# A Strassen stage's shared operands: four combinations moved to VectorE, four stores moved to SyncE, the plain half split first

## The chip, the cores and the metric

One core of one Trainium2 chip. The kernel computes a one-layer encoder trunk in fp32 accuracy. The metric is the device time of one execution in microseconds (us); the kernel before takes 1294.77 us in the median of three runs (1293.78 to 1295.44).

## The reference, cut to what matters

Tokens: 1024, plus 16 meta tokens; width 1024; FFN width 22 x 128 = 2816. The first half of the layer (RMSNorm, three token mixers, output projection, residual) is not touched by the change. The second half is

```python
a = rmsnorm(h, norm2)
h = h + (silu(a @ w_gate) * (a @ w_up)) @ w_down
out = rmsnorm(h, final_norm)
```

and the change lies in the operand `a` of the products with `w_gate` and `w_up`.

## The kernel before, in words

Every fp32 product is made of three fp32r products: each operand is split into a rounded part ("hi", a cast on ScalarE) and the rest ("lo", a subtraction of hi from the operand, on VectorE), and TensorE adds hi*hi, hi*lo and lo*hi. `product` (L890) does this for four blocks of 128 of the width, so one `product` is 12 matmuls of 128x512.

The activations of the FFN, transposed and scaled by `norm2`, lie in four fp32 tiles of 128 x 4 x 512: `bf[g, j]`, where g is the half of the width and j the half of the tokens. `turn_block(b)` (L740 on) makes the 128 tokens of block b: eight TensorE transposes (L744) of the normalised rows `hss[b]`, then two VectorE multiplications into `bf[0, j]` and `bf[1, j]` (L745). Blocks 4 to 7 (j = 1) come first, then blocks 0 to 3 (j = 0). `split_block(b)` makes hi (ScalarE, L751) and lo (VectorE, L752) of one block for both g; the parts are the tiles `bs[g, j]`.

Of the 22 chunks of 128 FFN columns, chunks 0 and 1 (`PAIR0`) are computed directly, `direct(c, j)`: gate and up, each `product` with `bs[0, j]` and then `bs[1, j]` into one PSUM bank of tag "s" (four banks), silu on ScalarE (L934), the multiplication with up on VectorE (L936), and a store of the result to DRAM (L924). It runs for j = 1 first, while blocks 0 to 3 are still being made, and for j = 0 afterwards. Chunks 2 to 21 go in pairs through `strassen`, seven products in place of eight on halves of the width and of the tokens. It needs, beside the plain parts `bs[0, 0]`, `bs[1, 0]`, `bs[1, 1]`, the parts t1, t2, t3, t4 of four combinations of the tiles `bf`:

- t3 = parts of bf[1,1] - bf[0,1]
- t1 = parts of bf[0,1] - bf[0,0], written in place over bf[0,1]
- t2 = parts of bf[1,1] - (the new bf[0,1]), in place over bf[1,1]
- t4 = parts of bf[1,0] - (the new bf[1,1]), in place over bf[1,0]

The four subtractions of 128 x 2048 run on GpSimd (L941, L949, L951, L953). `parts` makes hi with one cast of 128 x 2048 on ScalarE (L919) and lo with one subtraction of that size on VectorE (L920).

Where tiles lie sets what waits for what. `bs[g, 0]`, the tile of the t3 combination and the parts of t1, t2 and t3 are buffers of one tag "t" in the pool `rt`, which takes the memory of the closed pools `hp`, `x0` and `wo` (rows of the residual, normalised rows and weights of the stage before). The pool opens after block 3 has been transposed. The pool `po` of the Strassen part takes over the memory of the tiles `bf`; in it lie the raw weights of the second chunk of each pair, loaded by SyncE (L883). GpSimd adds and subtracts quarters of these raw weights (L989, L972), and ScalarE and VectorE split them (L876, L878).

The order on each engine is not written by hand. A planner goes through the program with its own estimate of each instruction's time and gives each engine the ready instruction that stands first in the program; the chip then runs each engine's list strictly in that order, and an instruction whose input is late holds up all that is behind it on its engine. A DMA is issued by the queue of the engine that the program names and waits there for its data in the same way. The buffers of one tag are handed out as the planner reaches their first writers.

Of the kernel before, what the change touches and what calls it, by code (L numbers as in the profile page):

```python
# [8 lines left out]
F32 = mybir.dt.float32  # L9
# [3 lines left out]
ALU = mybir.AluOpType  # L13
# [17 lines left out]
def hymba_trunk(  # L31
# [19 lines left out]
    nc = tc.nc  # L51
    V, S, G, PE = nc.vector, nc.scalar, nc.gpsimd, nc.tensor

    def pool(name, side=None, space=None, bufs=1):
        kw = {}
        if side is not None:
            kw["side"] = side
        if space is not None:
            kw["space"] = space
        return tc.tile_pool(name=name, bufs=bufs, reuse_waits="tile", **kw)  # L60
# [3 lines left out]
    def T(p, shape, dt, tag, bufs=1):  # L64
        uid[0] += 1
        return p.tile(list(shape), dt, tag=tag, bufs=bufs, name=f"{tag}_{uid[0]}")
# [689 lines left out]
    wts, bf, bs, hss, last_y = {}, {}, {}, {}, {}  # L756
# [3 lines left out]
    gsd = [dpool.tile([128, SEQ], F32, name=f"gsd{c}") for c in range(2)]  # L760
# [94 lines left out]
    g = len(OGROUPS) - 1  # L855
# [16 lines left out]
    HB = [128, 4, 512]  # L872
# [42 lines left out]
    rt = rt_stack.enter_context(pool("rt", side="right"))  # L915

    def parts(p, tag, bufs, a):
        hi, lo = [T(p, HB, F32R, tag, bufs) for _ in range(2)]
        S.copy(hi, a)  # L919
        V.tensor_tensor(lo, a, hi, ALU.subtract)  # L920
        return hi, lo

    def store(c, j, g):
        nc.scalar.dma_start(gsd[c][:, 512 * j:512 * j + 512], g)  # L924

    def direct(c, j):
        gu = []
        for m in range(2):
            p = mm("s", [128, 512], SB_)
            for kh in range(2):  # L930
                product(p, dw[c, m][kh], bs[kh, j], kh == 0)
            if m == 0:
                sg = T(wp, [128, 512], F32, "sg", 3)
                S.activation(sg, p, AF.Silu)  # L934
            else:
                V.tensor_tensor(sg, sg, p, ALU.mult)  # L936
        store(c, j, sg)


    t3f = T(rt, HB, F32, "t", 10)  # L940
    G.tensor_tensor(t3f, bf[1, 1], bf[0, 1], ALU.subtract)  # L941
    t3 = parts(rt, "t", 10, t3f)
    for g in range(2):
        bs[g, 0] = [T(rt, HB, F32R, "t", 10) for _ in range(2)]
    for b in range(4):
        split_block(b)
    for c in PAIR0:
        direct(c, 1)
    G.tensor_tensor(bf[0, 1], bf[0, 1], bf[0, 0], ALU.subtract)  # L949
    t1 = parts(rt, "t", 10, bf[0, 1])  # L950
    G.tensor_tensor(bf[1, 1], bf[1, 1], bf[0, 1], ALU.subtract)  # L951
    t2 = parts(rt, "t", 10, bf[1, 1])
    G.tensor_tensor(bf[1, 0], bf[1, 0], bf[1, 1], ALU.subtract)  # L953
    t4 = parts(e1, "s", 4, bf[1, 0])
    for c in PAIR0:
        direct(c, 0)
# [56 lines left out]
    for c0 in range(2, FF, 2):  # L1013
# [6 lines left out]
        for key, x in up.items():  # L1020
            g = gate[key]
# [158 lines left out]
```

## Time and profile before

| | |
|---|---|
| median of three runs | 1294.77 us |
| the profiled execution, own time | 1293.51 us |
| its span | 1291.7 us |
| mean granted TensorE clock | 0.977 of full speed |
| busy share of the span: PE, DVE, ACT, POOL | 94%, 73%, 49%, 39% |
| DMA, mean over the span | 114 GB/s |

PE is TensorE, DVE VectorE, ACT ScalarE, POOL GpSimd; SPq and ACTq are the queues in which SyncE and ScalarE issue DMAs. Times in rows count from the start of the span. "L751" is line 751 of the kernel. In a row of the timeline the bracket at the end says how long the engine stood idle before the instruction and what released it; "x8" after the shapes means that eight instructions are merged in the row. PEclk is the granted clock as a share of full speed (1.00 is 2.4 GHz, 0.50 is 1.2 GHz).

### The profile page before, as it was taken

The numbers are of one execution on the slowest core, as the hardware profiler recorded it, in microseconds if no ns is written. First come the engines' busy times: TensorE is split into PE (matmuls) and PEld (weight loads), VectorE is DVE, ScalarE is ACT, GpSimd is POOL, SyncE is SP. The second block draws the span as 40 slices with busy tenths as digits, with TensorE's granted clock in tenths as the row PEclk, the third lists the DMA queues.
The fourth block names the chain that finished last, engine by engine and source line by source line (L and its number), as shares of the span: only waits on it lengthen the run. The fifth ranks groups of instructions, "written<-read, shape, count | busy, mean of one in ns | idle before, by whom it ended". The sixth has DMA issues, their size and how long they took to land.

```text
span 1291.7 us, 18490 instructions
## 1 busy us (share of the span) xinstructions
PE 1218.8 (94%) x6310; PEld 1025.7 (79%) x6310; DVE 941.6 (73%) x1709; ACT 630.4 (49%) x1318; POOL 501.8 (39%) x538
## 2 busy tenths in 40 slices
PE   7799889999899989999979999999999999999997
PEld 6687778888788868777758888888888888788885
DVE  8667886868977679997657666666766655876557
ACT  6456754655548677668633233332323334444443
POOL 6459046362363774450355443344453410000001
PEclk9899899999998999999979999999999999999999
DMA  5100011010100161201505454345554449566653
GB/s 182 38 17 29 11 49 32 26 42 17 50 29 30 38 220 58 74 26 66 187 12 184 147 173 154 131 147 188 175 165 155 139 132 347 175 209 197 196 173 139
DMA packets 73146, 147.13 MB, mean 114 GB/s; under 512 B 9052, under 2 KB 21340, under 8 KB 73052
## 3 DMA queue, kind: packets, MB, share of 16 engines
q1 hardware_dynamic: 69152, 140.96, 33.0%
q10 hardware_dynamic: 3900, 4.99, 1.1%
q8 instruction: 50, 0.82, 0.3%
q14 instruction: 44, 0.36, 0.1%
HBM read 103.98 MB, written 41.94 MB: 113 GB/s over the span
## 4 chain that ended last, share of the span: by engine, by line
PE 70%; DVE 11%; DMA 3%; ACT 2%; issue 2%; POOL 0%; SPq 0%; DVEq 0%; ACTq 0%; POOLq 0%
PE s L890 24%; PE mm L289 10%; PE mm L890 8%; PE s L1075 7%; PE mm L701 4%; PE o L511 3%; PE mm L1075 3%; PE o L1075 3%; PE s L531 3%; DVE r L470 3%; PE s L429 1%; PE s L431 1%; DVE x L703 1%; DVE P L472 1%; DMA raw<-in_w_down 1%
## 5 line engine op out<-in xcount | busy, mean ns | idle before, releaser
L890 PE MATMUL s<-t,wh 128*128 128x512 f32 x544 | 171.6, 394 | 9.4 <-ACT t L751 5.3
L890 PEld LDWEIGHTS s<-t,wh 128*128 128x128 f32 x544 | 103.5, 190 | 32.1 <-ACT t L751 5.7
L890 PE MATMUL s<-s,wh 128*128 128x512 f32 x384 | 118.5, 390 | 0.0
L876 ACT CAST wh<-ss 128x512 fp32r<-128x512 f32 x80 | 49.6, 621 | 140.8 <-PE s L890 104.7
L890 PE MATMUL s<-t,wl 128*128 128x512 f32 x272 | 106.6, 392 | 0.0
L289 PE MATMUL mm<-x,wh 128*128 128x512 f32 (+1 forms) x320 | 100.0, 386 | 1.1 <-DVE pt L354 1.1
L538 ACT CAST ph<-s 128x512 fp32r<-128x512 f32 (+2 forms) x168 | 70.6, 434 | 60.0 <-PE s L531 23.9
L890 PE MATMUL mm<-t,wh 128*128 128x512 f32 x320 | 98.5, 389 | 0.0
L876 ACT CAST wh<-raw 128x512 fp32r<-128x512 f32 x68 | 41.7, 621 | 113.4 <-PE s L890 68.5
L1063 ACT CAST wh<-sg 128x512 fp32r<-128x512 f32 x74 | 46.0, 623 | 104.4 <-PE o L1075 46.0
L539 DVE TENSOR_TENSOR pl<-s,ph 128x512 fp32r<-128x512 f32 (+2 forms) x168 | 81.0, 492 | 19.6 <-ACT ph L538 17.4
L1064 DVE TENSOR_TENSOR wl<-sg,wh 128x512 fp32r<-128x512 f32 x74 | 51.0, 690 | 56.7 <-ACT wh L1063 56.5
L984 DVE TENSOR_TENSOR cg<-s,tmp 128x512 f32<-128x512 f32 x60 | 41.3, 689 | 62.4 <-PE s L890 62.4
L1114 POOL TENSOR_TENSOR r<-r,mhalf 128x1 f32<-128x1 f32 x8 | 4.4, 550 | 209.1 <-DVE r L1113 207.6
L511 PE MATMUL o<-pl,v 128*128 128x256 f32 (+1 forms) x288 | 84.7, 311 | 0.7 <-DVE pl L521 0.6
L890 PEld LDWEIGHTS s<-s,wh 128*128 128x128 f32 x384 | 71.9, 188 | 14.9
L511 PE MATMUL o<-ph,v 128*128 128x256 f32 (+1 forms) x288 | 79.2, 289 | 3.8 <-ACT ph L520 2.4
L289 PE MATMUL mm<-xa,wh 128*128 128x264 f32 (+3 forms) x248 | 79.9, 325 | 0.7 <-ACT rbc L239 0.4
L289 PE MATMUL mm<-xa,wl 128*128 128x264 f32 (+3 forms) x248 | 77.7, 318 | 1.2 <-POOL wl L164 1.2
L289 PE MATMUL mm<-xb,wh 128*128 128x264 f32 (+3 forms) x248 | 78.3, 318 | 0.0
L1022 POOL TENSOR_TENSOR cg<-cg,cg 128x512 f32<-128x512 f32 x30 | 46.8, 1559 | 76.3 <-DVE cg L984 70.8
L878 DVE TENSOR_TENSOR wl<-ss,wh 128x512 fp32r<-128x512 f32 x80 | 69.6, 875 | 7.0 <-ACT wh L876 6.1
(287 smaller groups left out, 3674.5 us busy)
## 6 DMA issues: line engine op xcount, KB each, us to landing
sg<-lsd SPq DMA_DIRECT2D x70, 256.0 KB, 3.3
raw<-in_w_gate SPq DMA_DIRECT2D x22, 512.0 KB, 5.2
raw<-in_w_up SPq DMA_DIRECT2D x22, 512.0 KB, 3.7
wr<-in_w_in SPq DMA_DIRECT2D x80, 128.0 KB, 2.3
raw<-in_w_down SPq DMA_DIRECT2D x20, 512.0 KB, 3.5
lsd<-cg SPq DMA_DIRECT2D x40, 256.0 KB, 3.3
raw<-rsd SPq DMA_DIRECT2D x40, 256.0 KB, 3.4
raw<-in_w_down SPq DMA_DIRECT2D x34, 256.0 KB, 3.1
```

Source lines behind the costliest of these rows:

```text
L289: PE.matmul(p[:, :n], w[k][ww], xx(k, t0, n), start=i == 0, stop=i == 23)
L511: PE.matmul(po[:, c:256], pr.v[h][:, kb, :], x, start=first and ix == 0, stop=(kb == nkb - 1 and ix == 1), skip_group_check=True)
L538: S.copy(ph[:, a:b], tpf[:, a:b])
L539: V.tensor_tensor(pl[:, a:b], tpf[:, a:b], ph[:, a:b], ALU.subtract)
L701: PE.matmul(p, y_[:, ts_], w_[:, ds], start=i == 0, stop=i == 3 * len(ws) - 1)
L876: S.copy(wh, a)
L878: V.tensor_tensor(wl, a, wh, ALU.subtract)
L890: PE.matmul(p, ws[ww][:, k, :], xs_[xx][:, k, :], start=first and i == 0, stop=i == 11, skip_group_check=True)
L1022: (V if key == (0, 0) else G).tensor_tensor(g, g, x, ALU.mult)
L1063: S.copy(wh, a)
L1064: V.tensor_tensor(wl, a, wh, ALU.subtract)
L1075: PE.matmul(p, x[xx][:, 128 * b:128 * b + 128], y[yy], start=first and i == 0, stop=last and i == 2, skip_group_check=True)
```

## The change

Three edits. The stores of the direct results are issued by SyncE in place of ScalarE. The four combinations run on VectorE in place of GpSimd. The combination t3 and its parts come behind the splits of blocks 0 to 3 and behind `direct(c, 1)` in the program, where they stood ahead of both; so the plain parts `bs[g, 0]` are now the first to ask for buffers of tag "t".

```diff
     def store(c, j, g):
-        nc.scalar.dma_start(gsd[c][:, 512 * j:512 * j + 512], g)
+        nc.sync.dma_start(gsd[c][:, 512 * j:512 * j + 512], g)
...
-    t3f = T(rt, HB, F32, "t", 10)
-    G.tensor_tensor(t3f, bf[1, 1], bf[0, 1], ALU.subtract)
-    t3 = parts(rt, "t", 10, t3f)
     for g in range(2):
         bs[g, 0] = [T(rt, HB, F32R, "t", 10) for _ in range(2)]
     for b in range(4):
         split_block(b)
     for c in PAIR0:
         direct(c, 1)
-    G.tensor_tensor(bf[0, 1], bf[0, 1], bf[0, 0], ALU.subtract)
+    t3f = T(rt, HB, F32, "t", 10)
+    V.tensor_tensor(t3f, bf[1, 1], bf[0, 1], ALU.subtract)
+    t3 = parts(rt, "t", 10, t3f)
+    V.tensor_tensor(bf[0, 1], bf[0, 1], bf[0, 0], ALU.subtract)
     t1 = parts(rt, "t", 10, bf[0, 1])
-    G.tensor_tensor(bf[1, 1], bf[1, 1], bf[0, 1], ALU.subtract)
+    V.tensor_tensor(bf[1, 1], bf[1, 1], bf[0, 1], ALU.subtract)
     t2 = parts(rt, "t", 10, bf[1, 1])
-    G.tensor_tensor(bf[1, 0], bf[1, 0], bf[1, 1], ALU.subtract)
+    V.tensor_tensor(bf[1, 0], bf[1, 0], bf[1, 1], ALU.subtract)
     t4 = parts(e1, "s", 4, bf[1, 0])
     for c in PAIR0:
         direct(c, 0)
```

## Rows read from the trace of the kernel before

**Rows 1.** Busy time by stretch: length, each engine's busy us, clock, DMA.
```profile
core 0: us, PE busy (x) PEld busy (x) DVE busy (x) ACT busy (x) POOL busy (x), PEclk, DMA share, GB/s
653.12:669.00 15.88, 6.47 (x15) 4.57 (x15) 13.23 (x11) 9.66 (x11) 8.69 (x3) 0.57 0.05 18
653.12:687.77 34.65, 25.24 (x97) 20.06 (x97) 23.74 (x20) 15.87 (x20) 22.42 (x7) 0.80 0.15 53
690.00:1100.00 410.00, 410.00 (x1810) 339.57 (x1810) 271.00 (x358) 130.69 (x222) 156.61 (x105) 1.00 0.51 173
```

**Rows 2.** TensorE in order of time: start, length, line, tiles; idle before.
```profile
652.89 0.39 PE L890 MATMUL s<-s,wl 128*128 128x512 f32 x1
658.56 2.07 PE L890 MATMUL s<-t,wh 128*128 128x512 f32 x4 [5.28 <-ACT t L751]
664.76 0.80 PE L890 MATMUL s<-t,wh 128*128 128x512 f32 x1 [4.13 <-DVE t L752]
665.35 0.63 PE L890 MATMUL s<-t,wl 128*128 128x512 f32 x1
...
666.63 0.63 PE L890 MATMUL s<-t,wl 128*128 128x512 f32 x1
...
687.77 0.62 PE L890 MATMUL mm<-t,wh 128*128 128x512 f32 x2
...
690.49 0.62 PE L890 MATMUL s<-t,wh 128*128 128x512 f32 x2
```

**Rows 3.** Waits of TensorE from 669 to the end: total, times, longest.
```profile
PE mm L1075 <- DVE wl L1064: 1.9, 1, 1.9
```

**Rows 4.** ScalarE in order of time.
```profile
646.98 0.60 ACT L934 ACTIVATE sg<-s 128x512 f32<-128x512 f32 x1 [7.62 <-PE s L890]
654.10 0.33 ACTq L924 DMA_DIRECT2D gsd<-sg  x1
654.53 1.90 ACT L919 CAST t<-t 128x2048 fp32r<-128x2048 f32 x1 [6.95 <-DVE sg L936]
656.33 4.26 ACT L751 CAST t<-f 128x512 fp32r<-128x512 f32 x8
...
683.73 1.14 ACT L876 CAST wh<-ss 128x512 fp32r<-128x512 f32 x2 [4.71 <-POOL ss L972]
```

**Rows 5.** VectorE in order of time.
```profile
650.14 1.29 DVE L745 TENSOR_TENSOR f<-o,n 128x512 f32<-128x512 f32 x2 [4.40 <-PE o L744]
653.38 0.69 DVE L936 TENSOR_TENSOR sg<-sg,s 128x512 f32<-128x512 f32 x1 [1.95 <-PE s L890]
656.46 5.84 DVE L920 TENSOR_TENSOR t<-t,t 128x2048 fp32r<-128x2048 f32 x1 [2.38 <-ACT t L919]
662.22 4.89 DVE L752 TENSOR_TENSOR t<-f,t 128x512 fp32r<-128x512 f32 x8
667.04 4.48 DVE L920 TENSOR_TENSOR t<-f,t 128x2048 fp32r<-128x2048 f32 x2
...
680.76 0.68 DVE L936 TENSOR_TENSOR sg<-sg,s 128x512 f32<-128x512 f32 x1
...
684.38 2.33 DVE L878 TENSOR_TENSOR wl<-ss,wh 128x512 fp32r<-128x512 f32 x3 [1.83 <-ACT wh L876]
```

**Rows 6.** GpSimd in order of time.
```profile
655.61 4.54 POOL L951 TENSOR_TENSOR f<-f,f 128x2048 f32<-128x2048 f32 x1
667.26 9.32 POOL L953 TENSOR_TENSOR f<-f,f 128x2048 f32<-128x2048 f32 x1 [7.11 <-DVE t L752]
680.25 1.75 POOL L989 TENSOR_TENSOR ss<-raw 128x512 f32<-128x512 f32 x1 [3.67 <-DMA raw<-in_w_gate]
682.07 1.62 POOL L972 TENSOR_TENSOR ss<-ss,raw 128x512 f32<-128x512 f32 x1
```

**Rows 7.** SyncE in order of time.
```profile
635.20 0.33 SPq L734 DMA_DIRECT2D hsd<-x  x1
676.60 0.33 SPq L883 DMA_DIRECT2D raw<-in_w_gate  x1
```

## The prediction

> **What bounds the kernel now.** I read first the busy time by stretch, because an average hides the one stage that the change touches. From 690 to 1100 us TensorE is busy for all of its 410 us at full clock [rows 1], and after 669 it waits for another engine once, for 1.9 us [rows 3]. So whatever is saved ahead of 669 reaches the end of the run, unless the Strassen part, which follows, finds its own inputs late. The stretch 653.12 to 669 is the opposite: TensorE works 6.47 of 15.88 us, at a mean granted clock of 0.57 [rows 1].
>
> TensorE's own order shows why. The last matmul of `direct(1, 1)` starts at 652.89, and since one starts every 0.227 us the next could start at 653.12. It starts at 658.56, after 5.28 us of idle that a cast of line 751 ends; four matmuls later come another 4.13 us that a subtraction of line 752 ends [rows 2]. Both are parts of `bs[0, 0]`, the plain half. From 653.12 to 687.77, where the first Strassen product starts (12 matmuls in 2.72 us, 0.2267 each [rows 2]), lie the two `direct(c, 0)`: 2 chunks x 2 matrices x 2 halves x 12 = 96 matmuls, 21.76 us at that pace. They take 34.65 [rows 1]. The excess is 12.89 us: 9.41 idle and 3.48 of matmuls at the lower clock (665.35 to 666.63 holds three, 0.427 each [rows 2]).
>
> Then the engines that make the parts. The data were there: block 3 leaves `turn_block` at 651.43 [rows 5], the other blocks earlier. But ScalarE, idle since 647.58, stands behind the second store, which waits for VectorE's sg; it issues at 654.10, the 1.90 us cast of t3 follows, and the eight casts of line 751 run from 656.33 to 660.59 [rows 4]. VectorE stands behind t3 too: its lo takes 5.84 us from 656.46, where the same subtraction takes 2.24 later, two in 4.48; only at 662.22 come the eight subtractions of line 752 [rows 5]. The casts thus followed t3 because the program put t3's buffers first.
>
> **Part by part.** *The plain half first* removes t3 from ahead of the plain parts. The buffers still open only once block 3 is transposed, so the planner must put the casts behind the silu that ends at 647.58 [rows 4]. On the chip three blocks of the first half then run at once (4.26/8 = 0.53 each), block 3 when its tile is there, at 650.14 + 0.65 = 650.8, to 651.4; the second half's four end at 653.6. VectorE ends line 745 at 651.43 and then does the eight lo at 0.60 each (4.89 for eight, the last one's end included [rows 5]): first half done at 653.9, second at 656.3. TensorE is free at 653.12. Its first matmul needs hi alone, and as before it can issue such matmuls into several banks (four at 658.56 [rows 2]), 0.23 us each. Wait: 0.1 to 0.7 us, I take 0.4. If the planner puts the multiplication of line 936 ahead of the eight lo, it runs from 653.38 to 654.07 [rows 5] and the first half ends at 656.5: 2.7 us of wait is the upper bound, 0 the lower. What was cover for these parts is the second half of `direct(1, 1)`; it has nothing left over, so each microsecond that line 745 slips is paid.
>
> *The combinations on VectorE.* GpSimd loses four: three like the 4.54 us row at 655.61 and one of 9.32 [rows 6]. No row shows this subtraction on VectorE; the nearest has the same 128x2048 shape with two SBUF inputs and another output type, 2.24 to 2.28 us. I take 2.28, 9.1 for four; the lower bound is 2.2, the upper 5.84, which the same row group shows beside GpSimd. The work of VectorE after 651.43 is then a queue: eight lo to 656.3, line 936 to 656.9, t3 combination 659.2, t1 combination 661.5 (beside ScalarE's 1.90 cast of t3), lo of t3 663.7, lo of t1 666.0, line 936 of chunk 0 at 666.6, t2 combination 668.9, t4 combination 671.2. Two lo follow, to 675.7. In all some 24 us in a stretch of 25, so VectorE takes the place of GpSimd as the engine that could be late. The t4 combination matters most: it is the last reader of the tile over which SyncE loads the second raw chunk. That load was issued at 676.60 [rows 7], as GpSimd ended the t4 combination (667.26 + 9.32 = 676.58), data came at 680.25, two GpSimd sums of 1.75 and 1.62 us follow [rows 6], a cast at 683.73 [rows 4] and the lo from 684.38 [rows 5], done at 685.0: 8.4 us from issue to the second Strassen product's weights. Before, the product came at 690.49 [rows 2], so this had 5.5 us of cover. Now it ends at 671.2 + 8.4 = 679.6, while TensorE arrives at 653.12 + 0.4 + 21.76 + 2.72 = 678.0. The cover is gone: 1.6 us of wait as far as nothing else is put there. The planner may bring the plain product with `bs[1, 0]` forward (0), or loads may come later (6 us and more, below). I take 1.5.
>
> *The stores.* Four issues of 0.33 us [rows 4] leave ScalarE and join SyncE, which issues nothing from 635.53 to 676.60 [rows 7]; the first two fall there and cost nothing. Behind the third and fourth stand the raw loads. The third has its data near 665, ahead of the loads at 671.2. The fourth has them at about 676. With the casts ahead of the store in ScalarE's order this edit alone is worth 0; if the store had stayed ahead of them it is worth up to the 5.28 us wait. I count 0.
>
> The sum: 12.89 - 0.4 - 1.5 = 11.0 us. The profiled execution took 1293.51 (its span of 1291.7 and 1.8 around it, which no edit touches), so 1282.5 are left; that execution is 1.26 below the median of the runs, so I predict 1283.8.
>
> **The rivals.** *The two engines share a port.* Rows: VectorE's 5.84 us lo began at 656.46, GpSimd's combination ended at 655.61 + 4.54 = 660.15, and 2.15 us after that the lo ended; GpSimd's 9.32 us one began at 667.26 and ended 5.06 us after VectorE's pair did at 671.52 [rows 5, 6]. Each stood still while the other ran. Here the first GpSimd sum at 674.8 would meet the last lo; if it must let both lo pass first, up to 4.6 us are added to 679.6, a wait of 6.2 at 678.0, and some 2 us of slow clock after it (here and below an estimate from the 3.48 that followed 9.41 of idle): 12.89 - 0.4 - 6.2 - 2 = 4.3 saved, 1290.5. For it: the two rows. Against: the lo end at 675.7, and one of the two is over when the data come. The Trainium skill (SBUF — State Buffer, section "SBUF: two separate sides") calls the pair of ports an exclusive lock, held for a whole instruction; by that rule the removal helps up to 671 and hurts behind it. The trace agrees, with 5.84 against 2.24. Chance 0.12.
>
> *The fourth store ahead of the raw loads* in SyncE's list: the loads would wait for chunk 1's last product (675.3) and line 936, to 676.1; weights at 684.5, a wait of 6.5 and 3 us of slow clock: 3 saved, 1291.8. For it: store and loads come ready within 5 us of each other in any estimate. Against: the loads' data are released first. Chance 0.10.
>
> *It does not do what it says*: the planner keeps the eight lo behind t3, since program order is not engine order. Then 654.07 + t3 and t1 combinations and lo of t3 (6.8) + 4.9 = 665.8 against 667.11: 1.3 saved, 1293.5. Chance 0.08.
>
> *Slower*: VectorE's list holds the late combinations behind line 936 of chunk 1. They start at 676.0, and t2 combination, one lo and t4 combination end at 682.9; weights at 691.3, wait 13.3, slow clock 3.5: 12.89 - 0.4 - 13.3 - 3.5 = -4.3, so 1299.1. It decides from a t4 combination that ends later than 678.6. For it: before, line 936 of chunk 0 came only at 680.76 [rows 5], behind the work for t4, so these orders do move. Against: VectorE's queue needs no more than 20 us to that point, TensorE 22. Chance 0.06.
>
> **How the numbers follow.** The forecast holds 0.62, with a range of its own from 1281.5 (nothing late) to 1286.5 (the late line 936 and a wait of 3). A further 0.02 is for a saving that a later wait eats. A difference of 0.2% is 2.6 us, about what can be told from none. Faster: forecast, port and store, 0.84; within: 0.10; slower 0.06. The range goes from 1281.0, just under the whole excess gone, to 1291.0, which takes in the port case and leaves out most of the store case and the two above it: 0.2 outside.
>
> **What would show it.** Right: TensorE's idle after 653.12 under 1 us and no stretch at 1.2 GHz behind it; line 751 from 647.6 and line 752 from 651.4; four VectorE rows of 2.2 to 2.3 us for the combinations; the raw load near 671; the first Strassen product near 675. Wrong: a wait of TensorE on line 876 or 878 of more than 3 us near 678, a raw load after 676, GpSimd sums well over 1.75 us, or line 752 still behind a 128x2048 subtraction.

## The result, and the profile after

The changed kernel takes 1285.36 us in the median (1283.81 to 1286.02, 4 runs), beside 1294.74 us for the kernel before on the same chip: ratio 0.9926, 95% interval 0.9909 to 0.9943, so 7.4 to 11.8 us less. Two later comparisons gave 0.9927 (0.9912 to 0.9942) and 0.9935 (0.9919 to 0.9952). The forecast was 1283.8.

The profiled execution of the changed kernel took 1286.02 us (span 1284.2), 7.49 less than that of before. The two executions can be compared stretch by stretch. First the busy time by stretch, for the first two stretches of [rows 1] and for one that the next reading needs:

```profile
core 0: us, PE busy (x) PEld busy (x) DVE busy (x) ACT busy (x) POOL busy (x), PEclk, DMA share, GB/s
653.12:669.00 15.88, 15.88 (x71) 12.88 (x70) 15.88 (x13) 7.18 (x6) 0.00 (x0) 1.00 0.05 18
653.12:687.77 34.65, 31.11 (x130) 24.77 (x129) 30.00 (x24) 14.10 (x16) 8.23 (x6) 0.95 0.21 71
681.40:685.67 4.27, 4.27 (x11) 3.17 (x12) 4.27 (x5) 2.94 (x6) 2.98 (x3) 0.60 0.00 0
```

From 653.12 to 669 TensorE is busy all the time at full clock, where it worked 6.47 us at 0.57. But so is VectorE: 15.88 of 15.88. In the longer stretch 3.54 us of idle and a mean clock of 0.95 are left. TensorE in order of time, answering to [rows 2], shows where:

```profile
652.98 1.28 PE L890 MATMUL s<-t,wh 128*128 128x512 f32 x4
...
674.97 0.62 PE L890 MATMUL mm<-t,wh 128*128 128x512 f32 x2
...
681.40 1.58 PE L890 MATMUL s<-t,wh 128*128 128x512 f32 x4 [3.54 <-ACT wh L876]
682.77 0.63 PE L890 MATMUL s<-t,wl 128*128 128x512 f32 x1
...
685.67 0.63 PE L890 MATMUL s<-t,wh 128*128 128x512 f32 x2
...
688.63 0.62 PE L890 MATMUL mm<-t,wh 128*128 128x512 f32 x2
```

The plain products start at 652.98 without a wait. The first Strassen product starts at 674.97, 12.80 us earlier than in [rows 2]. In front of the second one a new wait of 3.54 us has come, and the 11 matmuls from 681.40 to 685.67 take 4.27 us where 11 x 0.2267 = 2.49 would do: 1.78 more, at a mean granted clock of 0.60. From the first Strassen product to the first matmul of the down-projection (line 1075: at 1063.13 before, at 1055.83 after) the kernel before needs 375.36 us and the changed one 380.86, so 5.50 of the 12.80 are given back, nearly all of it here, and 7.30 are left.

VectorE in order of time, answering to [rows 5], holds the reason:

```profile
651.21 2.49 DVE L752 TENSOR_TENSOR t<-f,t 128x512 fp32r<-128x512 f32 x4
653.62 0.68 DVE L936 TENSOR_TENSOR sg<-sg,s 128x512 f32<-128x512 f32 x1
...
654.82 2.29 DVE L947 TENSOR_TENSOR t<-f,f 128x2048 f32<-128x2048 f32 x1
...
668.24 2.29 DVE L953 TENSOR_TENSOR f<-f,f 128x2048 f32<-128x2048 f32 x1
670.44 0.68 DVE L936 TENSOR_TENSOR sg<-sg,s 128x512 f32<-128x512 f32 x1
671.04 2.29 DVE L920 TENSOR_TENSOR t<-f,t 128x2048 fp32r<-128x2048 f32 x1
673.24 0.68 DVE L1038 TENSOR_TENSOR sg<-raw 128x512 f32<-128x512 f32 x1
673.84 2.28 DVE L920 TENSOR_TENSOR s<-f,s 128x2048 fp32r<-128x2048 f32 x1
676.04 0.68 DVE L936 TENSOR_TENSOR sg<-sg,s 128x512 f32<-128x512 f32 x1
681.38 2.31 DVE L878 TENSOR_TENSOR wl<-ss,wh 128x512 fp32r<-128x512 f32 x3 [4.66 <-ACT wh L876]
```

The order of the list is nearly the forecast's. The combination of t4 (line 953) ends at 670.53; then come line 936, the lo of t2 (line 920), which ends at 673.33, and a subtraction of the down-projection's weights (line 1038). What follows on SyncE and GpSimd, answering to [rows 7] and [rows 6], SyncE first:

```profile
673.95 0.32 SPq L1041 DMA_DIRECT2D rsd<-sg  x1
674.36 0.38 SPq L883 DMA_DIRECT2D raw<-in_w_gate  x1
...
676.75 0.33 SPq L924 DMA_DIRECT2D gsd<-sg  x1
```

```profile
678.09 1.26 POOL L989 TENSOR_TENSOR ss<-raw 128x512 f32<-128x512 f32 x1 [39.73 <-DMA raw<-in_w_gate]
679.43 1.26 POOL L972 TENSOR_TENSOR ss<-ss,raw 128x512 f32<-128x512 f32 x1
```

The raw load is issued at 674.36, not near 671.2. Its data release GpSimd 3.73 us later, two sums of 1.26 us follow, and the cast that TensorE waits for starts as the second one ends (680.69). The load is the late thing; what held it is the question for the experiments.

### The profile page after: what moved, and what is told of

Its sections match the earlier page's. It is cut to its first block, busy times and chain, and to the rows that moved or that the text cites. A ratio compares the mean times of both kernels' runs of the same rounds, so it can differ in the third digit from the quotient of the medians.

```text
span 1284.2 us, 18471 instructions
## 1 busy us (share of the span) xinstructions
PE 1215.3 (95%) x6310; PEld 1023.5 (80%) x6310; DVE 947.2 (74%) x1713; ACT 630.5 (49%) x1318; POOL 480.2 (37%) x534
## 4 chain that ended last, share of the span: by engine, by line
PE 66%; DVE 11%; issue 4%; ACT 4%; DMA 2%; POOL 1%; SPq 0%; DVEq 0%; POOLq 0%; ACTq 0%
PE s L890 21%; PE mm L289 10%; PE mm L890 8%; PE s L1075 7%; PE mm L701 4%; PE o L511 4%; PE mm L1075 3%; PE o L1075 3%; PE s L531 3%; DVE r L470 3%; PE s L429 1%; PE s L431 1%; DVE x L703 1%; DVE P L472 1%; DMA raw<-in_w_down 1%
## 5 line engine op out<-in xcount | busy, mean ns | idle before, releaser
L531 PE MATMUL s<-ident,P 128*128 128x128 f32 x432 | 68.8, 278 | 6.3 <-DVE pl L521 3.6
```

The source lines that it names most:

```text
L531: PE.transpose(tp[:, gi, ii, :], ptiles[ii][:, kc], ident)
```

## The experiments

The first three kernels each make one of the three edits alone.

**Order alone** (the plain half first; combinations still on GpSimd, stores on ScalarE). Against the changed kernel, the store and one of the four combinations:

```diff
-        nc.sync.dma_start(gsd[c][:, 512 * j:512 * j + 512], g)
+        nc.scalar.dma_start(gsd[c][:, 512 * j:512 * j + 512], g)
...
-    V.tensor_tensor(t3f, bf[1, 1], bf[0, 1], ALU.subtract)
+    G.tensor_tensor(t3f, bf[1, 1], bf[0, 1], ALU.subtract)
```

> Only the order is changed: the plain half's parts first, combinations on GpSimd and stores on ScalarE as before. If the order alone makes the gain and the engine of the combinations does not matter, this is as fast as the changed kernel, 1285 to 1286. My theory needs the engine too: the GpSimd combination of t3 starts near 650.5, as soon as block 3 is transposed, holds VectorE's two-input subtractions of line 752 out for its 4.55 us, and the four combinations with VectorE's own work between them end near 675 to 678, so that the raw load comes later than in the changed kernel. TensorE then waits 2 to 4 us near 654 and 5 to 8 us before the second Strassen product, with slow clock behind: 1289 to 1293, 2 to 6 us under the kernel before.

Measured: 1293.58 us (10 runs), ratio 0.9998 (0.9989 to 1.0008). No gain, where 2 to 6 us were expected. The longest wait of TensorE from 640 on (in total, times, longest), then VectorE and GpSimd in order of time:

```profile
PE s L890 <- DVE t L752: 8.3, 1, 8.3
...
```

```profile
650.18 10.86 DVE L752 TENSOR_TENSOR t<-f,t 128x512 fp32r<-128x512 f32 x4
...
661.56 2.48 DVE L752 TENSOR_TENSOR t<-f,t 128x512 fp32r<-128x512 f32 x4
```

```profile
649.81 4.58 POOL L949 TENSOR_TENSOR f<-f,f 128x2048 f32<-128x2048 f32 x1 [7.91 <-DVE f L745]
654.47 4.82 POOL L951 TENSOR_TENSOR f<-f,f 128x2048 f32<-128x2048 f32 x1
```

The plain parts do come first, but the multiplication of line 745 that lets them start also lets GpSimd's t1 combination start. GpSimd runs two combinations back to back to 659.29, and four subtractions of VectorE that take 2.48 us a little later take 10.86. A small part of the order's gain is there at first. Counted from the end of line 745, the first Strassen product starts after 36.34 us in the kernel before, after 33.66 here and after 23.67 in the changed kernel. But from that product to the down-projection this kernel needs 378.15 us, with waits of 1.25 and 0.86 us early in it, where the kernel before needs 375.36: the 2.7 us are given back. Most of what the order could give, the two engines' exclusion takes; the small rest is lost in the Strassen part.

**VectorE alone** (the four combinations of the kernel before on VectorE, nothing else; one of the four lines):

```diff
-    G.tensor_tensor(t3f, bf[1, 1], bf[0, 1], ALU.subtract)
+    V.tensor_tensor(t3f, bf[1, 1], bf[0, 1], ALU.subtract)
```

> Only the engine is changed: the four combinations on VectorE, in the old place in the program. If GpSimd's speed (4.54 us against 2.29) was what cost the time, 6 us or more are gained, 1288 or less. My theory: the plain parts still stand behind t3's chain on ScalarE and VectorE. From the rows, VectorE would do line 745 to 651.4, t3 combination to 653.6, line 936, t1 combination to 656.6, lo of t3 to 658.8, one lo of line 752, t2 combination, and the first half's lo end near 663.5, where they ended at 664.7 before. Gain 1 to 2 us: 1292.5 to 1294.

Measured: 1292.46 us (10 runs), ratio 0.999 (0.998 to 1.000): in the range expected, and hardly to be told from no change. VectorE in order of time:

```profile
651.03 2.28 DVE L941 TENSOR_TENSOR t<-f,f 128x2048 f32<-128x2048 f32 x1
...
653.83 2.28 DVE L949 TENSOR_TENSOR f<-f,f 128x2048 f32<-128x2048 f32 x1
656.03 2.28 DVE L920 TENSOR_TENSOR t<-t,t 128x2048 fp32r<-128x2048 f32 x1
658.24 0.68 DVE L752 TENSOR_TENSOR t<-f,t 128x512 fp32r<-128x512 f32 x1
658.84 2.28 DVE L951 TENSOR_TENSOR f<-f,f 128x2048 f32<-128x2048 f32 x1
661.04 4.29 DVE L752 TENSOR_TENSOR t<-f,t 128x512 fp32r<-128x512 f32 x7
```

Each instruction is at its free length now, but three of 2.28 us stand ahead of the first of line 752, and a fourth ahead of its other seven. TensorE waits 4.42 us for line 751 and 4.09 for line 752, much as before.

**Stores alone** (issued by SyncE, the rest as before):

```diff
-        nc.scalar.dma_start(gsd[c][:, 512 * j:512 * j + 512], g)
+        nc.sync.dma_start(gsd[c][:, 512 * j:512 * j + 512], g)
```

> Only the stores are moved to SyncE. If the stores' wait on ScalarE is the cause of the stall, the casts of t3 and of the plain half run from 647.5, and the gain is 8 us or more: 1286. If the store does not matter at all, 1294.7. My theory lies between: ScalarE is free, but on VectorE the lo of t3 still stands behind line 936 (to 654.0) and then meets a GpSimd combination; the first half's lo end near 660 instead of 664.7. Gain 3 to 6 us: 1289 to 1292.

Measured: 1294.01 us (10 runs), ratio 1.0005 (0.9993 to 1.0016). The casts come early, as expected, and nothing follows from it: ScalarE, then VectorE.

```profile
649.62 4.30 ACT L751 CAST t<-f 128x512 fp32r<-128x512 f32 x8
```

```profile
654.34 3.72 DVE L920 TENSOR_TENSOR t<-t,t 128x2048 fp32r<-128x2048 f32 x1
657.99 9.19 DVE L752 TENSOR_TENSOR t<-f,t 128x512 fp32r<-128x512 f32 x8
```

The eight lo, 4.89 us in [rows 5], take 9.19 beside GpSimd's t2 combination, and TensorE's two waits become one of 9.8 us for line 752.

**Without the stores** (the changed kernel, its stores on ScalarE again: order and VectorE):

```diff
-        nc.sync.dma_start(gsd[c][:, 512 * j:512 * j + 512], g)
+        nc.scalar.dma_start(gsd[c][:, 512 * j:512 * j + 512], g)
```

> The changed kernel with the four stores of the direct results issued by ScalarE again (order and VectorE kept). My theory: with the plain parts' casts ahead of the store in ScalarE's list, the store's place costs nothing: first Strassen product at 674 to 676 us, wait of TensorE on the casts of t4 or t2 3 to 4 us, median within 1.0 us of the changed kernel's (its own median beside it on this chip). The rival, that the stores are a third part without which the gain is not had (as neither order nor VectorE gained alone): casts of line 751 behind the second store from 654, wait of some 5 us in front of the plain products, 4 us or more above the changed kernel.

Measured: 1285.65 us (6 runs), ratio 0.9934 (0.9918 to 0.9949), beside 1284.80 and 0.9927 (0.9912 to 0.9942) for the changed kernel on that chip: the same. First Strassen product at 675.99, wait 3.5 us, 380.87 us to the down-projection. The store edit is worth nothing.

**Without the order** (VectorE and stores; the parts of t3 in their old place; one of the four combinations shown):

```diff
     def store(c, j, g):
-        nc.scalar.dma_start(gsd[c][:, 512 * j:512 * j + 512], g)
+        nc.sync.dma_start(gsd[c][:, 512 * j:512 * j + 512], g)
...
-    G.tensor_tensor(t3f, bf[1, 1], bf[0, 1], ALU.subtract)
+    V.tensor_tensor(t3f, bf[1, 1], bf[0, 1], ALU.subtract)
```

> The kernel before with two of the three edits: combinations on VectorE and stores issued by SyncE, but the plain half's parts in their old place behind those of t3. Theory (order and VectorE gain only together): the casts of line 751 run from 647 to 651 and TensorE starts at 653.1 with four matmuls, but VectorE's list still holds the t3 and t1 combinations and the lo of t3 (three times 2.28 us) ahead of most of line 752, so TensorE waits 7 to 10 us for line 752, and the median is 1291 to 1294, like VectorE alone (1292.46). Rival (without the two engines' exclusion the early casts are enough): wait under 4 us, first Strassen product before 680, 1286 to 1289.

Measured: 1293.0 us (10 runs), ratio 0.999 (0.9979 to 1.0002), as the theory had it, though not by its way. The casts were not early: the cast of t3 still stands ahead of them, and its combination on VectorE ends only at 652.60.

```profile
652.63 1.90 ACT L919 CAST t<-t 128x2048 fp32r<-128x2048 f32 x1 [6.08 <-DVE t L941]
654.44 4.25 ACT L751 CAST t<-f 128x512 fp32r<-128x512 f32 x8
```

TensorE waits 4.42 us for line 751 and 3.53 for line 752. So the five kernels with one or two edits fit one statement: order and VectorE together make the gain, and neither makes it alone. From the end of line 745 to the first Strassen product the order alone saves 2.7 us, VectorE alone 1.0, the stores alone 0.3, VectorE with the stores 0.7; order and VectorE save 12.7, with the stores or without. The order with the stores, the one pair left, was not run; in order alone the casts of line 751 are done at 652.41 and the store behind them is issued at 661.67, so no cast was seen to wait for it.

The other kernels ask what holds the raw load in the changed kernel.

**One store less ahead of the load** (the changed kernel, the first pair's store of line 1041 on ScalarE):

```diff
-        nc.sync.dma_start(rsd[5, c0], t1_)
+        (nc.scalar if c0 == 2 else nc.sync).dma_start(rsd[5, c0], t1_)
```

> The changed kernel with one more DMA moved: the store of the first down-projection combination (line 1041, first pair only) is issued by ScalarE. In the changed kernel it stands ahead of the raw loads in SyncE's list and is issued at 673.95, while the tile under the raw load is free at 670.5. My theory: the loads are then issued near 671.5, TensorE waits under 1.2 us instead of 3.5 before the second Strassen product and the 12 matmuls behind it run at full clock: 3.5 to 5.5 us under the changed kernel, 1280 to 1282. The rival, that VectorE's longer chain to the t4 combination or the load itself sets the wait: no change, 1285.4.

Measured: 1285.3 us (4 runs), ratio 0.993 (0.9913 to 0.9946): no gain, where 3.5 to 5.5 us were expected. The waits of SyncE's queue, and its issue:

```profile
SPq L883 <- DVE t L920: 1.8, 1, 1.8
```

```profile
672.47 0.33 SPq L883 DMA_DIRECT2D raw<-in_w_gate  x1
```

```profile
667.36 2.28 DVE L953 TENSOR_TENSOR f<-f,f 128x2048 f32<-128x2048 f32 x1
...
670.16 2.28 DVE L920 TENSOR_TENSOR t<-f,t 128x2048 fp32r<-128x2048 f32 x1
```

The third fence is VectorE's. The load is released by line 920, the lo of t2 (end 672.44), not by the combination of t4 (end 669.64). So the last reader of the tile under the raw load is the lo of t2, 2.8 us later than I had it; the store on SyncE's queue adds only 1.03 (in the changed kernel the load goes at 674.36, that lo ends at 673.33). TensorE's wait in front of the second product is 2.71 us, and the matmuls behind it run at a clock of 1.00; a new wait of 0.99 for line 979 takes part of that back. To the down-projection this kernel needs 379.87 us, 1.0 less than the changed one, and it loses that again further on (below).

**The early load** (the changed kernel, the second raw chunk's buffers in a pool of their own, so that they lie over none of the tiles `bf`):

```diff
-    rt = rt_stack.enter_context(pool("rt", side="right"))
+    rt = rt_stack.enter_context(pool("rt", side="right")); pr = rt_stack.enter_context(pool("pr", side="right"))
...
-        a10, a11 = raw_chunk(src, c0 + 1, po, "raw", 2)
+        a10, a11 = raw_chunk(src, c0 + 1, pr, "raw2", 2)
```

> The changed kernel with the second raw chunk's buffers in memory of their own, so that the load of the raw gate and up columns needs no reader of the tokens' halves to end first. Theory (the second Strassen product waits 3.54 us, and then loses 1.8 us to a lower clock, because its raw load waits for the lo of t2 at 673.3 to leave that memory): the raw load is issued before 650, TensorE's wait in front of the second Strassen product falls below 1 us, no stretch at half pace behind it, and the median is 4 to 5.5 us under the changed kernel's: 1280 to 1281.5 if that is 1285.4. Rival A (the sums and casts of these weights are late by themselves, behind the lo of t4 and the line 936 in VectorE's list): the load is early, the wait stays at 2 us or more on VectorE, under 2 us gained. Rival B (what is saved there is given back at the down-projection's start, where the clock falls): the second product starts at 678 or before, and the median is within 1.5 us of the changed kernel's.

and a second time, on another chip:

> The changed kernel with the early load once more, beside the changed kernel, because the first comparison (1283.9 against 1284.8, intervals overlapping) did not separate them while its trace is 3.5 us shorter from the first Strassen product to the down-projection. If those 3.5 us reach the end: 2 to 4 us under the changed kernel's median here. If they are given back at the down-projection's start, whose clock fell in two of the faster kernels: within 1.5 us of it, with a mean clock in the profile's stretch 1090 to 1110 below 1.00.

> The changed kernel itself once more, on the same chip as the runs beside it: the median that they are compared with. If the earlier result holds, 1284 to 1287 us and 7 to 11 us under the kernel before; the wait in front of the second Strassen product 3 to 4 us again with its raw load issued between 673 and 676, as the order of the program fixes it.

> The changed kernel on the same chip as the runs beside it, for their comparison: 1284 to 1287; if the spread of single runs is the down-projection's start and the stages ahead of the change, its stretch from the first Strassen product to the down-projection is again 380.9 us in the profile, as in the two profiles so far.

Measured: 1283.92 us (6 runs), ratio 0.9914 (0.9898 to 0.9929), beside 1284.80 for the changed kernel; then 1281.67 (4 runs), ratio 0.9901 (0.9883 to 0.9919), beside 1285.49 (0.9919 to 0.9952). In the first comparison the intervals overlap, in the second they touch at 0.9919. Over both, ten runs of the early load have their median at 1282.0, the sixteen runs of the changed kernel, its first four included, at 1285.2: some 3 us, less than the 4 to 5.5 expected. The traces agree: from the first Strassen product to the down-projection 377.38 and 377.70 us, where three profiles of the changed kernel have 380.86, 380.95 and 380.91. So the load's place in memory is shown to cost 3.2 to 3.6 of the 5.3 us. TensorE and GpSimd of the first of these two kernels:

```profile
675.89 0.62 PE L890 MATMUL mm<-t,wh 128*128 128x512 f32 x2
...
680.25 1.25 PE L890 MATMUL s<-t,wh 128*128 128x512 f32 x4 [1.48 <-ACT wh L876]
```

```profile
674.38 3.82 POOL L989 TENSOR_TENSOR ss<-raw 128x512 f32<-128x512 f32 x1 [35.10 <-DVE t L920]
```

A wait of 1.48 us remains, against my "below 1". The load is there long before (issued at 634.34), but the sum of line 989 waits for the same lo of t2, since its own buffer lies in that memory too, and then takes 3.82 us instead of 1.26 beside the lo of t4. Of the run's rivals, A (late by themselves) does not hold as it stood, with 2 us or more on VectorE and under 2 us gained; but the rest of 1.48 us is of its kind, with GpSimd's sum in place of VectorE's list. B (given back later) would fit the 0.9 us of the first comparison, not the 3.8 of the second, and the clock from 1090 to 1110 is 1.00 in both profiles.

**Both early** (the buffers of the sums first in their pool as well, so that they lie over a tile that is free sooner):

```diff
-    for _ in range(10):
-        T(po, [128, 512], F32, "cg", 10)
+    for i in range(13):
+        T(po, [128, 4, 128] if i < 3 else [128, 512], F32, *(("ss", 3) if i < 3 else ("cg", 10)))
```

> As the run with the early load, and the three buffers of the weights' sums put first in their pool as well, so that these no longer lie over the half that the lo of t2 reads last but over the other one, which is free earlier. Theory: if in the run with only the early load the sums still start behind the lo of t2 (673.3), they start 2 us or more earlier here, the second Strassen product has no wait at all, and the median is 0 to 1 us under that run's, 4.5 to 6 us under the changed kernel's. Rival (the lists of VectorE and ScalarE, not the memory, set when those weights are ready): the same as the run with only the early load within 0.7 us, the sums no earlier.

Measured: 1284.11 us (6 runs), ratio 0.9913 (0.9895 to 0.9931): no better than the early load alone. GpSimd and ScalarE:

```profile
667.75 3.22 POOL L989 TENSOR_TENSOR ss<-raw 128x512 f32<-128x512 f32 x1 [30.08 <-DVE t L920]
671.06 3.22 POOL L972 TENSOR_TENSOR ss<-ss,raw 128x512 f32<-128x512 f32 x1
```

```profile
677.19 0.58 ACT L994 COPY tmp<-mm 128x512 f32<-128x512 f32 x1 [4.40 <-PE mm L890]
677.67 1.66 ACT L876 CAST wh<-ss 128x512 fp32r<-128x512 f32 x3
```

The two sums that TensorE waits for are done at 674.28, and still it waits 1.19 us: their casts stand behind the copy of line 994, which waits for the end of the first Strassen product. The rival (the lists) is right, though the sums did come earlier. And a little later two new waits come, for an addition on VectorE:

```profile
PE s L890 <- DVE tmp L979: 1.6, 2, 1.2
```

From the first Strassen product to the down-projection this kernel needs 379.25 us, more than the early load alone.

**The copy on VectorE** (as before, and line 994 of the first gate pair made by VectorE):

```diff
-        S.copy(u1, p)
+        (V.tensor_copy if (src is w_gate and c0 == 2) else S.copy)(u1, p)
```

> As the run with both buffers early, and the copy of the first Strassen product (line 994) of the first gate pair made by VectorE in place of ScalarE. Theory: what was left of the wait in front of the second product (1.19 us) is ScalarE's list: its casts of the weights' sums, whose data were there at 675.98, stand behind the copy, which waits for the first product's end at 677; without it in that list the wait falls below 0.4 us and nothing runs at the low clock behind it. Median 0.5 to 2 us under the run with both buffers early (1284.1), as far as nothing is lost at the down-projection's start, where that run's profile lost 2 us to the clock. Rival (the wait moves to VectorE, where the copy now stands ahead of line 878): a wait of 0.8 us or more on VectorE, median the same within 0.7.

Measured: 1285.1 us (6 runs), ratio 0.9927 (0.9908 to 0.9946). The theory fails, and its rival holds for the wait, though the median lies 1.0 us above that of both early, taken on another chip, and not within 0.7: the second product starts at 677.53 with no wait for its hi, and stops after four matmuls.

```profile
677.53 1.07 PE L890 MATMUL s<-t,wh 128*128 128x512 f32 x4
680.52 0.50 PE L890 MATMUL s<-t,wl 128*128 128x512 f32 x1 [1.92 <-DVE wl L878]
```

VectorE's list is full there (lo of t4 stretched to 3.38 us by GpSimd's sums, line 936, the copy), so the wait changed its owner. To the down-projection it is 378.91 us.

A second loss came to these two kernels, and to the run with one store less, further on. Busy time from 1090 to 1110, at the start of the down-projection, in the early load and in both early:

```profile
1090.00:1110.00 20.00, 18.27 (x81) 14.81 (x80) 16.00 (x26) 7.69 (x13) 0.00 (x0) 1.00 0.61 200
```

```profile
1090.00:1110.00 20.00, 17.97 (x73) 14.35 (x72) 15.36 (x25) 6.97 (x13) 0.00 (x0) 0.91 0.55 183
```

Nearly the same time is busy, with 8 matmuls fewer. In the profiles of one store less, both early and the copy on VectorE the clock there is 0.91, and the stretch from the first matmul of line 1075 to the last takes 221.2 to 221.6 us; in all profiles of the changed kernel and of the early load it is 1.00, and 219.4 to 219.8. The wait for line 1064 in that stretch is 1.7 to 2.1 us in all of them. The length of the wait does not decide it: it is 1.9 to 2.0 us in the three, and in order alone (2.25) and in VectorE with the stores (2.49) the clock stayed at 1.00. Why it falls in some and not in others is open.

## Why the prediction was right, and where it was not

*What bounds the kernel, the plain half first: right.* The excess of 12.89 us ahead of the first Strassen product went as worked out: predicted wait 0.4, measured none; predicted start 675.3, measured 674.97. The lo of the first half ended at 653.70, the forecast's 653.9, and line 936 came behind it, not ahead.

*The combinations on VectorE: right in price, incomplete in worth.* Four rows of 2.29 us, where 2.28 was taken. The rival of the shared port did not come: GpSimd's sums took 1.26 us, since their data came at 678.09, when VectorE was idle. But I priced the removal from GpSimd only by what it adds to VectorE, and told the port's part of it in a rival alone. The runs with one edit show that the gain needs the removal as much as the order. With GpSimd's combinations in place, the earlier lo would only have run into them (10.86 us for four). My expectations for order alone (1289 to 1293) and for stores alone (1289 to 1292) missed for this reason. The Trainium skill (SBUF — State Buffer, section "SBUF: two separate sides") says that a VectorE operation with two SBUF inputs and a GpSimd operation that reads SBUF lock each other out for a whole instruction. The traces here agree: 10.86 against 2.48, 9.19 against 4.89, and, the other way round, 3.82 against 1.26.

*The wait in front of the second Strassen product: the term that was mis-sized.* I had 1.5 us and nothing for the clock; it was 3.54, and 1.78 of lower clock behind it, 5.3 together. By the prediction's own signs, a wait on line 876 of more than 3 us and a stretch at a lower clock, this part was wrong. The step that failed is the one on the t4 combination: "it is the last reader of the tile over which SyncE loads the second raw chunk". In the kernel before that combination came last, because GpSimd was slow with it and the lo of t2 was done at 671.52 [rows 5, 6]. In VectorE's list the lo of t2 comes behind it, by a line 936 and 2.29 us, and the run with one store less shows the load released by it. My own queue had this lo next; I did not ask which of the two the load would wait for. So the load went 3.16 us later than forecast (674.36 against 671.2). The rest of the chain took less than the 8.4 us taken: from issue to data 3.73 (3.65 in [rows 6, 7]), two sums of 1.26 in place of 1.75 and 1.62, and TensorE started with the hi alone, 7.04 us behind the issue. That shorter chain hid some 1.4 us of the late load; without it the wait would have been near 5.

*The stores: right in sum, wrong in one place.* Worth 0 in all three runs that bear on it (alone, left out, with VectorE). The fourth store stood behind the loads, as forecast; another store, of line 1041, which the prediction did not count, stood ahead of them, for 1.0 us.

*The sum.* 12.80 gained, 5.50 given back by the start of the down-projection, 0.19 gained behind it: 7.49 between the two profiled executions, where I had 11.0. The medians differ by 9.4. The profiled execution of the changed kernel is the slowest of its four, and single runs spread by some 4 us (1283.8 to 1288.2); between its three profiles the first Strassen product starts at 674.97, 676.70 and 676.67, so part of that spread lies ahead of the change. I take the 7.49 for what the trace accounts for; some 2 us of the medians' difference stand in no row. So the median came nearer to the forecast than the working did, and that nearness is luck. The range of the forecast's own case does not come out of its terms either: the whole excess gone gives 1294.77 - 12.89 = 1281.9, not 1281.5, and the late line 936 with a wait of 3 gives 12.89 - 2.7 - 3 = 7.2 saved, 1287.6, not 1286.5.

The slower rival, the late t4 combination, asked for an end later than 678.6; it ended at 670.53.

## What to carry to other kernels

Where two engines shut each other out, as in order alone, an edit that only brings one's work forward gains little as long as the other's long instruction is released by the same event; look at the releaser of both before pricing either. When work moves between engines, the order of the last readers of a buffer moves with it: list all readers of the memory under a late load in the new order, and take the last, not the one that was last before. And each wait taken away was replaced by one of a neighbour on a full list: of the 5.3 us the first of three edits got back 3.2 to 3.6 by the start of the down-projection, and with the second and the third added to it the kernels got back less, 1.6 and 2.0.

## What the runs showed of the hardware that was not expected

Two engines that shut each other out can take turns, instruction by instruction. In order alone GpSimd's second combination stands 0.08 us behind the first (649.81 + 4.58, then 654.47), and still one of VectorE's short subtractions got between them. The first two of the four, singly:

```profile
650.18 4.75 DVE L752 TENSOR_TENSOR t<-f,t 128x512 fp32r<-128x512 f32 x1
```

```profile
654.86 4.98 DVE L752 TENSOR_TENSOR t<-f,t 128x512 fp32r<-128x512 f32 x1
```

The first ends at 654.93, 0.54 us behind the first combination, and the second at 659.84, 0.55 behind the second one; the other two take 0.68 each. So the 10.86 us are two subtractions that each stood still for one GpSimd instruction, and the profile counts that time as busy. VectorE's rows do not always let GpSimd in: in the early load GpSimd's sum passed behind line 1038 and the lo of t4 as well (3.82 us, ending 1.15 behind that lo), while in both early the sums (3.22 us each) and VectorE's subtractions took turns. What decides between the two is open.

A lower clock behind a wait of TensorE comes in some kernels only. At the down-projection's start it was 0.91 in three, for some 2 us of difference, and 1.00 in the others named above behind the same wait. In front of the second Strassen product it was 0.60 behind 3.54 us and 1.00 behind 2.71 us.
